# Two sums in two banks for the convolution's taps, in a decoder layer that runs at TensorE's pace

## The chip, the core and the metric

The kernel runs on one core of one Trainium2 chip. The metric is the device time of one execution in microseconds. In the profile PE is TensorE's matmuls and PEld its weight loads, DVE is VectorE, ACT ScalarE, POOL GpSimd, SP SyncE.

## What is computed

One decoder layer on a sequence of 512 positions with 1024 features: a half-step feed-forward layer, a token mixer, a second half-step feed-forward layer and a gated embedding. The mixer joins a sliding-window attention with a convolution branch. The change lies in the branch's depthwise convolution, 31 taps back in time, each channel by itself:

```python
ca, cb = jnp.split(zc, 2, axis=-1)
u = ca * jax.nn.sigmoid(cb)
u = causal_depthwise_conv(u, dw_w[i], dw_b[i])
c = jax.nn.silu(layernorm(u, conv_ln_g[i], conv_ln_b[i])) @ conv_proj[i]
...
merged = jax.nn.sigmoid(ga) * a + jax.nn.sigmoid(gb) * c
x = x + merged @ w_out[i]
```

For a feature f the convolution is y[f, s] = b[f] + sum over d from 0 to 30 of w[30 - d, f] * u[f, s - d], with zeros ahead of the sequence.

## The kernel before

Activations lie feature by position: eight tiles of 128 features (partitions) by 512 positions, called channels 0 to 7 below. A weight matrix comes in pieces of 128x1024, each split into a high and a low part by ScalarE and VectorE (`whi_`, `wlo_`), and each product takes three matmuls (high times high, low times high, high times low). A projection of one output tile is thus 24 matmuls of 512 columns into one PSUM bank.

The kernel is first recorded and then planned. `record()` writes the program down as operations on named tiles without places. `simulate()` then plays the operations through with a cost for each (`costs`) and gives every tile a place and every operation a start; `plan()` does this several times with different due times and keeps the shortest. Each engine then gets its instructions in the order of those starts (`hybrid_layer`, where line 1778 issues all of them, so that every row of the profile bears that line). A change to some operations thus makes a new order for all engines, and the order is fixed once the kernel is built. The written list `ORDER` gives the sequence in which the mixer's steps are recorded: `a` and `b` are the two projections of a convolution channel (tiles `ca`, `cb`), `K` and `Q` keys, values and queries, `A`, `E`, `V` scores, softmax and values of a query block, `g` and `h` the two gates (`ga`, `gb`), `p` the attention's output projection (`ap`), `L` the normalization behind the convolution. The projection `cp` reads what `L` leaves. The queries of the first eight heads come from `query_unit` with the seven-product form of `unit` and turned operands (tiles `wq_a`, `wq_b`), the other eight from a plain projection (`q1b`).

PSUM has eight banks, each 128 x 512 float32, class `ps` in the planner. A projection holds one while it sums, a group of scores takes four at once (`sc`), each transpose (`qTp`, `pT`) one, the plain query projection four.

The convolution of a channel starts when its gate is through (`conv_gate`, which makes `u`). Channels 0, 2 and 4 (`POOLCH`) are summed by GpSimd in SBUF, with ScalarE scaling each tap (tiles `ct`). Channels 1, 3, 5, 6 and 7 are summed by VectorE in a PSUM bank (`cz`): tap 0 with the bias by a `tensor_scalar`, taps 2 to 30 each by a `scalar_tensor_tensor` that reads the bank and writes it back, a copy of column 0, and at last tap 1, whose result goes to the SBUF tile `ys`. The class of `cz` tiles has a limit of two banks in use (`CAPS`). A tile can have a `mate`; the planner then opens both together:

```python
need.setdefault(vt.cls, {})[vt] = True
if vt.mate:
    need[vt.cls][vt.mate] = True
...
if len(free[c]) < len(vts) + spare:
    return False
if any(vt.kind and inuse[vt.kind] + (vt.mate is not None) >= CAPS[vt.kind] for vt in vts):
    return False
```

`conv_norm` (step `L`) adds the eight `ys` tiles (`ln_acc`), splits the sum (`ln_s`), takes the mean over features with a matmul (`ln_mb`), then the variance (`ln_v`), and splits the normalized tiles for `cp` (`cv_h`, `cv_l`).

Of the kernel before, what the change touches and what calls it, by code (L numbers as in the profile page):

```python
# [9 lines left out]
F32 = mybir.dt.float32  # L10
F32R = mybir.dt.float32r
I32 = mybir.dt.int32
AF = mybir.ActivationFunctionType
ALU = mybir.AluOpType
AX = mybir.AxisListType

P = 128
S = 512
# [10 lines left out]
TAPS = 31  # L29
PAD = TAPS - 1  # L30
# [14 lines left out]
POOLCH = (0, 2, 4)  # L45
# [643 lines left out]
def record():  # L689
    nc = Program()  # L690
# [4 lines left out]
    def ftile(name):  # L695
        return nc.tile(name, [P, S], F32, "a")
# [205 lines left out]
    g_ffn1, g_mix, g_ffn2, g_gate, g_ple, dwb, lng, lnb = (g_all[:, i] for i in range(8))  # L902
# [32 lines left out]
    dww = nc.tile("dww", [P, KD, TAPS], F32, "c")  # L935
# [301 lines left out]
    def halves(tag, key, i, h, cuts):  # L1237

        w = piece(key, i)
        out = []  # L1240
        for c in range(cuts):
            v = slice(c * S // cuts, (c + 1) * S // cuts)
            out.append(ps_tile(f"{tag}_{c}"))
            with nc.group(f"{tag}_{c}"):
                for k in range(KD):
                    mm3(out[c][:, v], part(w, slice(k * P, (k + 1) * P)), part(h[k], v), k == 0, k == KD - 1)
        return out
# [14 lines left out]
    us, ys, pas = [None] * KD, [None] * KD, [None] * KD  # L1262
# [4 lines left out]
    def conv_gate(c):  # L1267
        pb = proj(f"cb{c}", "wzc", 2 * c + 1, h2)
        sg = ftile(f"sg{c}")
        nc.vector.tensor_tensor(sg, pb, rb2, op=ALU.mult)  # L1270
        nc.scalar.activation(sg, sg, AF.Sigmoid)
        nc.gpsimd.tensor_tensor(sg, sg, rb2, op=ALU.mult)
        us[c] = ftile(f"u{c}")
        nc.vector.tensor_tensor(us[c], pas[c], sg, op=ALU.mult)
        conv(c)
# [3 lines left out]
    def conv(c):  # L1279
        u = us[c]  # L1280
        ys[c] = ftile(f"y{c}")
        ext = c not in POOLCH
        y = nc.tile(f"cz{c}", [P, S], F32, "ps") if ext else ys[c]
        nc.vector.tensor_scalar(
            y, u, dww[:, c, PAD:TAPS], dwb[:, c : c + 1], op0=ALU.mult, op1=ALU.add
        )
        for d in [*range(2, TAPS), 1] if ext else range(1, TAPS):
            wk = dww[:, c, PAD - d : TAPS - d]
            yd, ud = y[:, d:S], u[:, 0 : S - d]
            if not ext:  # L1290
                t = ftile(f"ct{c}_{d}")[:, 0 : S - d]
                nc.scalar.activation(t, ud, AF.Copy, scale=wk)
                nc.gpsimd.tensor_tensor(yd, yd, t, op=ALU.add)
            elif d == 1:
                nc.vector.tensor_copy(ys[c][:, 0:1], y[:, 0:1])
                nc.vector.scalar_tensor_tensor(ys[c][:, d:S], ud, wk, yd, op0=ALU.mult, op1=ALU.add)
            else:
                nc.vector.scalar_tensor_tensor(yd, ud, wk, yd, op0=ALU.mult, op1=ALU.add)


    def heads_rsqrt(tag, zs, n, scale, psum):
# [392 lines left out]
    for oo in range(1):  # L1694
# [6 lines left out]
        for f, m, b1, b2 in steps:  # L1701
            o = 2 * oo + m
            if f == 1:
                t, u = gt[m] = ftile(f"gt{o}"), ftile(f"gt{o + 4}")
# [4 lines left out]
            elif f == 6:  # L1709
                t, u = gt[m]  # L1710
                nc.scalar.copy(t[:, hi_], b2)
                nc.scalar.copy(u[:, hi_], b1)
            elif f == 7:
                t, u = gt[m]
# [6 lines left out]
            else:  # L1721
                t, u = gt[m]
                nc.vector.scalar_tensor_tensor(u[:, lo_], b2, -1.0, rb4[:, lo_], op0=ALU.mult, op1=ALU.mult)
                gate(o + 4, u, lo_)
    for i, o in enumerate((2, 3, 6, 7)):
        ps = halves(f"pg{o}", "wgate", 4 + i, h4, 2 if o == KD - 1 else 1)
# [169 lines left out]
```

## Time and profile before

| what | value |
|---|---|
| median of 3 runs | 1145.6 us (1145.52 to 1145.76) |
| profiled execution | 1145.5 us, span 1143.8 us |
| busy PE / PEld | 1135.7 / 1054.2 us |
| busy DVE / ACT / POOL | 1000.4 / 743.0 / 457.8 us |
| mean granted TensorE clock | 0.999 |
| the taps on VectorE | from 389.8 to 618.8 us of the span |

Busy time of an engine is the time in which it has at least one instruction in execution. Matmul records overlap, so the pitch from one matmul's start to the next says more than PE's busy share. Times in the lists below are microseconds from the span's start; a row of the timeline gives the start, the duration (of a run of like instructions where it ends in xN), the engine and the operation, and in brackets how long the engine sat idle before it and what ended that.

### The profile page before, as it was taken

The numbers are of one execution on the slowest core, as the hardware profiler recorded it, in microseconds if no ns is written. First come the engines' busy times: TensorE is split into PE (matmuls) and PEld (weight loads), VectorE is DVE, ScalarE is ACT, GpSimd is POOL, SyncE is SP. The second block draws the span as 40 slices with busy tenths as digits, with TensorE's granted clock in tenths as the row PEclk, the third lists the DMA queues.
The fourth block names the chain that finished last, engine by engine and source line by source line (L and its number), as shares of the span: only waits on it lengthen the run. The fifth ranks groups of instructions, "written<-read, shape, count | busy, mean of one in ns | idle before, by whom it ended". The sixth has DMA issues, their size and how long they took to land.

```text
span 1143.8 us, 20799 instructions
## 1 busy us (share of the span) xinstructions
PE 1135.7 (99%) x7804; PEld 1054.2 (92%) x7804; DVE 1000.4 (87%) x1701; ACT 743.0 (65%) x1332; POOL 457.8 (40%) x531
## 2 busy tenths in 40 slices
PE   9999999999999999999999999999999999999998
PEld 8899999999999988888888888988999999999997
DVE  7799978889887799997997779989998788899897
ACT  7656456665557889999975654655663566565682
POOL 1632113322112896976688124035231132131156
PEclk9999999999999999999999999999999999999999
DMA  7456666665658481664644554436666666656643
GB/s 242 126 162 148 165 160 163 151 144 151 157 132 208 119 206 38 173 158 97 162 129 131 146 148 108 114 108 169 145 164 151 150 167 148 168 119 178 152 117 99
DMA packets 54821, 167.92 MB, mean 147 GB/s; under 512 B 6592, under 2 KB 14400, under 8 KB 54720
## 3 DMA queue, kind: packets, MB, share of 16 engines
q1 hardware_dynamic: 39888, 114.12, 30.2%
q0 software_dynamic: 14688, 52.44, 26.6%
q8 instruction: 61, 1.00, 0.4%
q14 instruction: 40, 0.33, 0.1%
q10 hardware_dynamic: 144, 0.03, 0.0%
HBM read 145.59 MB, written 2.10 MB: 129 GB/s over the span
## 4 chain that ended last, share of the span: by engine, by line
PE 97%; DVE 3%; issue 0%; ACT 0%; ACTq 0%
PE wgu_b L1778 17%; PE wgu_a L1778 13%; PE wd_b L1778 10%; PE wd_a L1778 8%; PE f_g L1778 5%; PE f_u L1778 5%; PE gb L1778 4%; PE ga L1778 4%; PE ap L1778 4%; PE cp L1778 4%; PE ca L1778 3%; PE cb L1778 3%; PE wout_b L1778 2%; PE pg L1778 2%; PE q1b L1778 2%; PE wout_a L1778 2%
## 5 line engine op out<-in xcount | busy, mean ns | idle before, releaser
L1778 DVE TENSOR_TENSOR wlo_wgu<-raw_wgu,whi_wgu 128x1024 fp32r<-128x1024 f32 (+1 forms) x141 | 140.4, 1010 | 27.1 <-ACT whi_wgu L1778 26.8
L1778 ACT ACTIVATE whi_wgu<-raw_wgu 128x1024 fp32r<-128x1024 f32 (+1 forms) x141 | 115.4, 838 | 69.8 <-PE wgu_b L1778 34.7
L1778 POOL TENSOR_TENSOR y<-y,ct 128x511 f32<-128x511 f32 (+26 forms) x90 | 112.0, 1319 | 14.1 <-ACT ct L1778 5.3
L1778 PE MATMUL wgu_b<-f_t_h,wlo_wgu 128*128 128x256 f32 x408 | 115.5, 283 | 0.0
L1778 PE MATMUL wgu_b<-f_t_h,whi_wgu 128*128 128x256 f32 x408 | 115.5, 283 | 0.0
L1778 PE MATMUL wgu_b<-f_t_l,whi_wgu 128*128 128x256 f32 x408 | 115.5, 283 | 0.0
L1778 ACT ACTIVATE whi_wd<-raw_wd 128x896 fp32r<-128x896 f32 (+1 forms) x60 | 59.3, 989 | 73.3 <-PE wd_b L1778 41.5
L1778 DVE SCALAR_TENSOR_TENSOR cz<-u,dww,cz 128x504 f32<-128x504 f32 (+28 forms) x145 | 104.7, 733 | 2.0
L1778 POOL DMA_DIRECT2D raw_wgu<-in_wgu x34 | 29.7, 878 | 153.3 <-DMA raw_wgu<-in_wgu 78.6
L1778 PEld LDWEIGHTS wgu_b<-f_t_h,wlo_wgu 128*128 128x128 f32 x408 | 78.3, 192 | 0.0
L1778 PEld LDWEIGHTS wgu_b<-f_t_h,whi_wgu 128*128 128x128 f32 x408 | 78.3, 192 | 0.0
L1778 PEld LDWEIGHTS wgu_b<-f_t_l,whi_wgu 128*128 128x128 f32 x408 | 78.3, 192 | 0.0
L1778 DVE TENSOR_TENSOR wlo_wd<-raw_wd,whi_wd 128x896 fp32r<-128x896 f32 (+1 forms) x60 | 70.8, 1180 | 7.2 <-ACT whi_wd L1778 6.8
L1778 PE MATMUL wgu_a<-f_nh,wlo_wgu 128*128 128x256 f32 x272 | 77.0, 283 | 0.0
L1778 PE MATMUL wgu_a<-f_nh,whi_wgu 128*128 128x256 f32 x272 | 77.0, 283 | 0.0
L1778 PE MATMUL wgu_a<-f_nl,whi_wgu 128*128 128x256 f32 x272 | 77.0, 283 | 0.0
L1778 PE MATMUL wd_b<-f_f_h,wlo_wd 128*128 128x256 f32 x264 | 75.1, 285 | 1.2 <-DVE x L1778 1.2
L1778 PE MATMUL wd_a<-f_f_h,wlo_wd 128*128 128x256 f32 x264 | 74.7, 283 | 0.0
L1778 PE MATMUL wd_a<-f_f_h,whi_wd 128*128 128x256 f32 x264 | 74.7, 283 | 0.0
L1778 PE MATMUL wd_b<-f_f_l,whi_wd 128*128 128x256 f32 x264 | 74.7, 283 | 0.0
L1778 PE MATMUL wd_b<-f_f_h,whi_wd 128*128 128x256 f32 x264 | 74.7, 283 | 0.0
L1778 PE MATMUL wd_a<-f_f_l,whi_wd 128*128 128x256 f32 x264 | 74.7, 283 | 0.0
(625 smaller groups left out, 4278.6 us busy)
## 6 DMA issues: line engine op xcount, KB each, us to landing
raw_wgu<-in_wgu SPq DMA_DIRECT2D x76, 512.0 KB, 4.5
raw_wgu<-in_wgu POOLq DMA_DIRECT2D x34, 512.0 KB, 5.5
raw_wd<-in_wd SPq DMA_DIRECT2D x32, 448.0 KB, 4.0
raw_wd<-in_wd SPq DMA_DIRECT2D x16, 512.0 KB, 4.4
raw_wzc<-in_wzc SPq DMA_DIRECT2D x16, 512.0 KB, 3.9
wlo_wzc<-raw_wzc POOLq DMA_DIRECT2D x16, 512.0 KB, 4.9
raw_wzg<-in_wzg SPq DMA_DIRECT2D x16, 512.0 KB, 3.5
wlo_wzg<-raw_wzg POOLq DMA_DIRECT2D x16, 512.0 KB, 4.5
```

What stands on the lines that cost most here:

```text
L1778: made[op] = getattr(engines[op.eng], op.what)(*a, **k)
```

## The change

The five VectorE channels get two PSUM tiles each, `ya` and `yb`, mates of each other. Even taps go to `ya` (tap 0 opens it with the bias), odd taps to `yb` (tap 1 opens it by a `tensor_scalar` with 0 added), in the order 0, 1, 2, 4, 5, ... 30, 3. Tap 3, the last, writes its result to `ys` instead of the bank. Then two small copies bring columns 1 and 2 of `yb` and column 0 of `ya` into `ys`, and a `tensor_tensor` adds `ya` to `ys`. A channel has 34 instructions in place of 32. The branch for channels 0, 2 and 4 is written out apart, with the same operations as before. With a limit of two `cz` banks, mates can only be opened when no other channel holds one.

```diff
     def conv(c):
         u = us[c]
         ys[c] = ftile(f"y{c}")
-        ext = c not in POOLCH
-        y = nc.tile(f"cz{c}", [P, S], F32, "ps") if ext else ys[c]
-        nc.vector.tensor_scalar(
-            y, u, dww[:, c, PAD:TAPS], dwb[:, c : c + 1], op0=ALU.mult, op1=ALU.add
-        )
-        for d in [*range(2, TAPS), 1] if ext else range(1, TAPS):
+        if c in POOLCH:
+            y = ys[c]
+            nc.vector.tensor_scalar(y, u, dww[:, c, PAD:TAPS], dwb[:, c : c + 1], op0=ALU.mult, op1=ALU.add)
+            for d in range(1, TAPS):
+                t = ftile(f"ct{c}_{d}")[:, 0 : S - d]
+                nc.scalar.activation(t, u[:, 0 : S - d], AF.Copy, scale=dww[:, c, PAD - d : TAPS - d])
+                nc.gpsimd.tensor_tensor(y[:, d:S], y[:, d:S], t, op=ALU.add)
+            return
+        ya, yb = (nc.tile(f"cz{c}{n}", [P, S], F32, "ps") for n in "ab")
+        ya.vt.mate, yb.vt.mate = yb.vt, ya.vt
+        for d in [*range(3), *range(4, TAPS), 3]:
+            y = (ya, yb)[d % 2]
             wk = dww[:, c, PAD - d : TAPS - d]
             yd, ud = y[:, d:S], u[:, 0 : S - d]
-            if not ext:
-                t = ftile(f"ct{c}_{d}")[:, 0 : S - d]
-                nc.scalar.activation(t, ud, AF.Copy, scale=wk)
-                nc.gpsimd.tensor_tensor(yd, yd, t, op=ALU.add)
+            if d == 0:
+                nc.vector.tensor_scalar(yd, ud, wk, dwb[:, c : c + 1], op0=ALU.mult, op1=ALU.add)
             elif d == 1:
-                nc.vector.tensor_copy(ys[c][:, 0:1], y[:, 0:1])
-                nc.vector.scalar_tensor_tensor(ys[c][:, d:S], ud, wk, yd, op0=ALU.mult, op1=ALU.add)
+                nc.vector.tensor_scalar(yd, ud, wk, 0.0, op0=ALU.mult, op1=ALU.add)
             else:
-                nc.vector.scalar_tensor_tensor(yd, ud, wk, yd, op0=ALU.mult, op1=ALU.add)
+                to = ys[c][:, d:S] if d == 3 else yd
+                nc.vector.scalar_tensor_tensor(to, ud, wk, yd, op0=ALU.mult, op1=ALU.add)
+        nc.vector.tensor_copy(ys[c][:, 1:3], yb[:, 1:3])
+        nc.vector.tensor_copy(ys[c][:, 0:1], ya[:, 0:1])
+        nc.vector.tensor_tensor(ys[c][:, 1:S], ya[:, 1:S], ys[c][:, 1:S], op=ALU.add)
```

## The prediction

> **What bounds the kernel now.** I read the page's first part and its chain first, then the windows of the stage in which the convolution runs, then what the weight loads of TensorE waited for.
>
> ```profile
> span 1143.8 us, 20799 instructions
> PE 1135.7 (99%) x7804; PEld 1054.2 (92%) x7804; DVE 1000.4 (87%) x1701; ACT 743.0 (65%) x1332; POOL 457.8 (40%) x531
> PE 97%; DVE 3%; issue 0%; ACT 0%; ACTq 0%
> ...
> L1778 DVE TENSOR_SCALAR cz<-u,dww,g_all x5: 799/803/806, 389.8 to 584.9; 128x512 f32<-128x512 f32 x5
> L1778 DVE COPY y<-cz x5: 157/157/159, 393.2 to 593.3; 128x1 f32<-128x1 f32 x5
> L1778 DVE SCALAR_TENSOR_TENSOR y<-u,dww,cz x5: 729/742/747, 436.0 to 618.1; 128x511 f32<-128x511 f32 x5
> ...
> 389.70:618.80 229.10, 227.96 (x1227) 190.41 (x1226) 214.20 (x386) 206.37 (x431) 184.07 (x239) 1.00 0.56 139
> 389.70:618.80 229.10, 112.52 (x160) 1.00 0.56 139
> ```
>
> The tile view of `cz` dates the stage: the first tap starts at 389.8, the last ends just before 618.8. In the windows over it (columns: PE, PEld, DVE, ACT, POOL, clock, DMA share, GB/s) PE is busy 227.96 of 229.10 us and VectorE 214.20, of which the second row, the same window for `cz` alone, gives the taps 112.52. So VectorE is the second busiest engine here, but the chain is 97% TensorE. Busy matmul records overlap, so I look at the pitch in the chain instead.
>
> ```profile
> 460.67 21.79 PE q1b L1778 x96
> 576.70 5.44 PE ga L1778 x24
> 661.10 43.52 PE cp L1778 x192
> ```
>
> 43.52/192 is 0.227 us for a matmul 512 wide; in the stage 5.44/24 and 21.79/96 are the same 0.227. TensorE runs at its own pace beside the taps, and what it loses stands in its waits:
>
> ```profile
> PEld wd_b L1778 <- DVE x L1778: 2.1, 4, 0.7
> PEld sc L1778 <- issue: 1.4, 4, 0.4
> PEld ca L1778 <- DVE s L1778: 1.1, 1, 1.1
> PEld sc L1778 <- DVE cz L1778: 0.4, 1, 0.4
> PEld pT L1778 <- POOL s L1778: 0.3, 1, 0.3
> PEld cb L1778 <- DVE s L1778: 0.3, 1, 0.3
> ```
>
> Three waits in the stage can go: `ca` 1.1, `cb` 0.3, `pT` 0.3, together 1.7 us. The `sc` waits, 0.4 us each whoever is named (the `cz` row is one of them), come before score groups and follow no particular engine; I leave them. `wd_b` lies outside the stage. **So a faster convolution has 1.7 us to win in its own stage, 0.15% of the run.** A difference of 0.2% (2.3 us) is about what a measurement of this kernel tells from no change.
>
> **The change part by part.** Before, five channels (1, 3, 5, 6, 7) each sum 31 taps in one bank; a tap reads what the tap before it wrote. What that costs is seen by comparing two runs of taps. Channel 3 opens only at 417.37, so the run at 401.50 is one channel in one bank; at 475.95 channels 3 and 5 take turns in two.
>
> ```profile
> 401.50 5.40 DVE L1778 SCALAR_TENSOR_TENSOR cz<-u,dww,cz 128x502 f32<-128x502 f32 x7
> 417.37 0.80 DVE L1778 TENSOR_SCALAR cz<-u,dww,g_all 128x512 f32<-128x512 f32 x1
> 473.57 0.80 DVE L1778 TENSOR_SCALAR cz<-u,dww,g_all 128x512 f32<-128x512 f32 x1
> 475.95 6.46 DVE L1778 SCALAR_TENSOR_TENSOR cz<-u,dww,cz 128x486 f32<-128x486 f32 x10
> ```
>
> With 0.74 us for the last record of each, same bank: (5.40 - 0.74)/6 = 0.777 us from start to start; by turns: (6.46 - 0.74)/9 = 0.636. The dependence costs 0.14 us a tap. It costs that only where a tap directly follows a tap of its own bank; behind any other instruction the wait is already covered. I count 60 such followers in the stage, the first and the last of them in these rows:
>
> ```profile
> 390.60 0.76 DVE L1778 SCALAR_TENSOR_TENSOR cz<-u,dww,cz 128x510 f32<-128x510 f32 x1
> 618.05 0.75 DVE L1778 SCALAR_TENSOR_TENSOR y<-u,dww,cz 128x511 f32<-128x511 f32 x1
> ```
>
> Removed: with turns, one same-bank follower is left in each channel (tap 4 behind tap 2), so 55 x 0.14 = 7.7 us of VectorE time go.
>
> Added to each channel: a second TENSOR_SCALAR in place of a tap, one more small COPY, and the closing addition of the two sums. The addition reads one bank and one SBUF tile and writes SBUF, like `u<-ca,sg`:
>
> ```profile
> 393.24 0.16 DVE L1778 COPY y<-cz 128x1 f32<-128x1 f32 x1
> 393.43 0.75 DVE L1778 SCALAR_TENSOR_TENSOR cz<-u,dww,cz 128x508 f32<-128x508 f32 x1
> 415.94 0.68 DVE L1778 TENSOR_TENSOR u<-ca,sg 128x512 f32<-128x512 f32 x1
> 416.54 0.18 DVE L1778 SCALAR_TENSOR_TENSOR q_y<-q_rs,q_y 128x32 f32<-128x32 f32 x1
> 584.92 0.80 DVE L1778 TENSOR_SCALAR cz<-u,dww,g_all 128x512 f32<-128x512 f32 x1
> 585.64 2.65 DVE L1778 SCALAR_TENSOR_TENSOR cz<-u,dww,cz 128x483 f32<-128x483 f32 x4
> ```
>
> From start to start: addition 416.54 - 415.94 = 0.60, TENSOR_SCALAR 585.64 - 584.92 = 0.72 less the tap it replaces 0.64, copy 393.43 - 393.24 = 0.19. That is 0.60 + 0.08 + 0.19 = 0.87 a channel; the addition may also wait 0.14 for the copy before it. Five channels: 4.4 us, at most 5.1. Tap 3 writing to `ys` instead of the bank is the old last tap's form (742 ns in the tile view), no change.
>
> Net on VectorE: 4.4 - 7.7 = **-3.3 us** in 229 (-2.6 with the extra waits, +4.4 if turns gained nothing). On the path: nothing directly, since TensorE's 228 us cover it. If that cover were gone the gain would be at most the 1.7 us of waits. POOL and ScalarE do the three other channels as before; no DMA and no matmul is added or removed.
>
> The Trainium skill, Advanced Engine Details and Errata, The Read-Write Bubble, says that memory latency shows as a bubble between instructions, and makes no difference between banks. By that rule alone the turns would save nothing and VectorE's sum would be +4.4 instead of -3.3; the trace here, 0.777 against 0.636, speaks for a part that depends on the bank.
>
> What the change takes is room. A channel now opens two of the eight banks together, and the code lets it open only when no other channel holds one. Before, one bank was held from 389.8 to 618.8, and two only while neighbours overlapped:
>
> ```profile
> 435.99 0.75 DVE L1778 SCALAR_TENSOR_TENSOR y<-u,dww,cz 128x511 f32<-128x511 f32 x1
> 482.32 0.74 DVE L1778 SCALAR_TENSOR_TENSOR y<-u,dww,cz 128x511 f32<-128x511 f32 x1
> 589.45 0.73 DVE L1778 SCALAR_TENSOR_TENSOR y<-u,dww,cz 128x511 f32<-128x511 f32 x1
> ```
>
> That is 417.37 to 436.7, 473.57 to 483.1, 584.92 to 590.2: 34 us. After, two are held nearly all the time. A group of scores takes four banks at once, and PE's order is fixed, so a missing bank stops everything behind the group. No row shows such a wait as it will be. Below it may be a gain: the three waits go, -1.7. Above, each of the eight score groups waits once as `ca` does at 428.83, for the copies out of score banks:
>
> ```profile
> 428.34 0.77 DVE L1778 COPY_PREDICATED s<-masks,sc 128x256 f32<-128x256 int32 x2
> 428.83 0.19 PEld L1778 LDWEIGHTS ca<-mix_h_h,wlo_wzc 128*128 128x128 f32 x1 [1.12 <-DVE s L1778]
> ```
>
> 8 x 1.1 = +8.8. The copies that free a score bank are short, and six banks hold four scores, a transpose and a projection; so I take the low side, one wait like that of `cb`, +0.3.
>
> **The sum.** The profiled execution took 1145.5 us (span 1143.8 and 1.7 around it), the three runs have a median of 1145.6. 1145.6 + 0 (taps, covered) + 0.3 = 1145.9 us.
>
> **The rivals.**
> *Slower: score groups wait for banks.* For it: the order of the whole kernel is worked out anew at build from a model of costs, with one bank fewer for TensorE in this stage, and the order before leaves TensorE so little idle time that any new order is more likely to add than to take. Against it: with two channels open, 417 to 437, TensorE still kept its pace outside the one wait. It decides from the third wait of 1.1 us on (2.3 us in all); four of them give 1150.0, eight 1154.4. The Trainium skill, Perfetto Trace Analysis, Matmul Optimizations, wants all eight banks in use for parallel work of TensorE, which speaks for this rival.
>
> *Slower: the channels end late.* A channel waits until two banks are free together and the channel before has ended, so the last sum may come late for the normalization:
>
> ```profile
> 618.83 0.69 DVE L1778 TENSOR_TENSOR ln_acc<-ln_acc,y 128x512 f32<-128x512 f32 x1
> 625.00 0.69 DVE L1778 TENSOR_TENSOR ln_s_l<-ln_acc,ln_s_h 128x512 fp32r<-128x512 f32 x1 [3.74 <-ACT ln_s_h L1778]
> 630.94 0.39 PE L1778 MATMUL ln_mb<-ln_s_h,mean_r 128*128 128x512 f32 x1
> 662.67 1.30 DVE L1778 TENSOR_TENSOR cv_l<-y,cv_h 128x512 fp32r<-128x512 f32 x2 [0.24 <-ACT cv_h L1778]
> ```
>
> The sum's split is ready at 625.7 and its matmul comes at 630.9: 5.2 us of slack. Behind it there is little, the last `cv_l` ends at 664.0 when `cp` has run since 661.1. Each us beyond 5.2 is idle TensorE time; a last sum 10 us late gives 4.8, so 1150.4, and from 7.5 us late it decides. Against it: channels 6 and 7 hold many of the 60 followers and become shorter.
>
> *Faster.* VectorE's shorter queue removes all three waits: 1145.6 - 1.7 = 1143.9, still within 0.2%. More needs also the `wd_b` waits outside the stage (2.1): 1141.8. Nothing in the change reaches them but the new order.
>
> *The change doesn't do what it says.* If turns within one channel keep the pitch of 0.777, VectorE has 4.4 us more in a stage where it idles 229.1 - 214.2 = 14.9: again 1145.9, with a wait or two.
>
> **How the numbers follow.** Same, with or without the tap gain: 0.56 (0.46 and 0.10). Banks: 0.26. Late end: 0.12. Faster by over 0.2%: 0.06. So faster 0.06, same 0.56, slower 0.38, and the time is that of the same case, 1145.9, whose own range is 1143.9 to 1147.9. The range reaches down to 1143.9 (three waits gone), leaving 0.07 below, and up to 1151.5, five waits of 1.1 and a little more, leaving 0.12 above.
>
> **What would show it.** Taps at a pitch near 0.64 us with no run at 0.78; 170 records in the five channels against 160 (34 each: 2 TENSOR_SCALAR, 29 taps, 2 copies, 1 addition); VectorE in the stage some 3 us less busy; TensorE's 0.227 unchanged. The banks' rival would show as waits of `sc` or the projections above 0.4 us on VectorE's or ScalarE's reads of scores; the late end as idle TensorE before `ln_mb` or `cp`. I am wrong if the stage's waits of PEld for other engines come to 4 us or more, or if TensorE loses time in a stage that has no taps because the new order is worse there.

## The result, and the profile after

The changed kernel takes 1152.79 us (median of four runs, 1152.54 to 1153.1), the kernel before beside it 1145.67 (1145.52 to 1145.76). The ratio is 1.0062 with a 95% interval of 1.0045 to 1.008: slower by 7.1 us. The forecast was 1145.9 with a range up to 1151.5, and no difference as the likeliest case; the time lies 1.3 us above that range.

First the lines of the page that answer to those of before (span; busy time of the engines; chain of work that ended last):

```profile
span 1150.8 us, 20811 instructions
PE 1138.3 (99%) x7804; PEld 1054.0 (92%) x7804; DVE 1003.0 (87%) x1711; ACT 748.3 (65%) x1336; POOL 456.6 (40%) x531
PE 86%; DVE 6%; ACT 6%; issue 0%; DMA 0%; ACTq 0%; DVEq 0%
```

TensorE has the same 7804 matmuls and is 99% busy by its records as before, but its share of the chain fell from 97% to 86%, and 6% each went to VectorE and ScalarE: the chain now passes through them. These shares are not TensorE's waits, which come to a few us and are read below. The place is found by the start of `cp` in the chain of the changed kernel:

```profile
668.18 43.52 PE cp L1785 x192
```

Before it was 661.10, with the same 43.52 us. So the whole loss (7.0 us of span, 7.08 by this row) lies ahead of `cp`, and what follows is unchanged. The windows (columns PE, PEld, VectorE, ScalarE, GpSimd, clock, DMA share, GB/s) narrow it down; before:

```profile
0.00:389.80 389.80, 388.05 (x2865) 371.80 (x2866) 331.64 (x588) 235.39 (x423) 111.90 (x145) 1.00 0.62 159
389.80:450.00 60.20, 59.06 (x367) 50.38 (x366) 59.39 (x118) 54.88 (x121) 48.98 (x68) 1.00 0.59 142
450.00:500.00 50.00, 50.00 (x267) 41.51 (x266) 46.67 (x85) 49.65 (x99) 45.73 (x65) 1.00 0.57 141
500.00:570.00 70.00, 70.00 (x384) 57.99 (x381) 61.46 (x125) 69.32 (x167) 45.37 (x71) 1.00 0.58 141
```

and after:

```profile
0.00:389.80 389.80, 387.96 (x2864) 371.63 (x2865) 331.81 (x587) 235.10 (x423) 111.91 (x145) 1.00 0.62 159
389.80:450.00 60.20, 59.38 (x369) 50.56 (x368) 59.81 (x119) 53.84 (x109) 51.49 (x68) 1.00 0.58 143
450.00:500.00 50.00, 46.67 (x230) 37.32 (x230) 49.44 (x86) 49.64 (x106) 45.48 (x66) 1.00 0.52 125
500.00:570.00 70.00, 68.63 (x385) 56.21 (x384) 59.37 (x119) 68.70 (x164) 47.68 (x73) 1.00 0.57 138
```

Up to the first tap nothing differs. From 450 to 500 TensorE lacks 3.3 us and from 500 to 570 1.4 us, where before it lacked none. Idle records are not the whole loss: a matmul can start late while the record before it still runs, since the records overlap. For every matmul I took the time to the next one's start, less the usual pitch of its shape (0.227 us for 512 columns, 0.120 for 256, 0.109 for a transpose). From 400 to 600 us the sum of this excess is 7.0 us larger after than before; 4.9 of it stands behind transposes (`pT`, `qTp`), 1.9 behind matmuls 512 wide.

The waits of TensorE in the stage (what waited, for whom, us, times, longest) were one row before:

```profile
PE ca L1778 <- DVE s L1778: 0.9, 1, 0.9
```

After there are nine, 5.4 us together, all of which follow:

```profile
PE pT L1785 <- ACT zq L1785: 1.0, 1, 1.0
PE o L1785 <- DVE sgb L1785: 0.9, 1, 0.9
PE qTp L1785 <- DVE of L1785: 0.8, 1, 0.8
PE qTp L1785 <- DVE q_rs L1785: 0.6, 1, 0.6
PE pT L1785 <- DVE s L1785: 0.6, 2, 0.3
PE cb L1785 <- DVE of L1785: 0.5, 1, 0.5
PE q1b L1785 <- DVE s L1785: 0.4, 1, 0.4
PE ca L1785 <- DVE s L1785: 0.4, 1, 0.4
PE o L1785 <- DVE p_l L1785: 0.2, 1, 0.2
```

Read each row by whether the named result is an operand. `pT` transposes `s`, not `zq`; `qTp` and `cb` don't read `of`; `q1b` and `ca` don't read `s`; `o` does not read `sgb`. What these have in common is that the named instruction reads a PSUM bank (`zq` reads `q1b`, `sgb` reads `gb`, `of` reads `o`, `s` reads `sc`), and the matmul that waits is the next to write in a bank. Six rows, 4.0 us, are thus what a wait for a bank looks like. The plan of the changed kernel says which bank each tile has (`vt.slot`), and it confirms them: in each of the six rows the tile that waits opens the bank that the named instruction is the last to read. By the same numbers the row `pT` <- `s` belongs to them, although `pT` does read `s`: both times the transposes open a bank of scores from another query block. That makes 4.6 us. The other two rows (`q_rs`, `p_l`), 0.8 us, fit operands of the queries and of the softmax that come late. One of the first kind in the timeline:

```profile
484.07 1.82 ACT L1785 ACTIVATE zq<-q1b,mix_n_r 128x512 f32<-128x512 f32 x3
484.88 1.20 PE L1785 MATMUL pT<-ident,s 128*128 128x128 f32 x8 [0.99 <-ACT zq L1785]
```

ScalarE empties the query projection's banks, and the transposes begin when one of them is read.

### The profile page after: what moved, and what is told of

Read it like the earlier page. It is cut to its first block, busy times and chain, and to the rows that moved or that the text cites. A ratio compares the mean times of both kernels' runs of the same rounds, so it can differ in the third digit from the quotient of the medians.

```text
span 1150.8 us, 20811 instructions
## 1 busy us (share of the span) xinstructions
PE 1138.3 (99%) x7804; PEld 1054.0 (92%) x7804; DVE 1003.0 (87%) x1711; ACT 748.3 (65%) x1336; POOL 456.6 (40%) x531
## 4 chain that ended last, share of the span: by engine, by line
PE 86%; DVE 6%; ACT 6%; issue 0%; DMA 0%; ACTq 0%; DVEq 0%
PE wgu_b L1785 17%; PE wgu_a L1785 13%; PE wd_b L1785 10%; PE wd_a L1785 8%; PE f_g L1785 5%; PE f_u L1785 5%; PE ap L1785 4%; PE cp L1785 4%; PE gb L1785 3%; PE ga L1785 2%; ACT s L1785 2%; PE wout_b L1785 2%; PE ca L1785 2%; PE pg L1785 2%; PE cb L1785 2%; PE wout_a L1785 2%
## 5 line engine op out<-in xcount | busy, mean ns | idle before, releaser
L1785 POOL TENSOR_TENSOR y<-y,ct 128x505 f32<-128x505 f32 (+27 forms) x90 | 111.0, 1270 | 14.6 <-ACT ct L1785 7.6
L1785 POOL TENSOR_TENSOR f_f_ta<-f_us 128x256 f32<-128x256 f32 x22 | 25.5, 1161 | 96.9 <-DVE f_us L1785 79.9
```

What stands on the lines that cost most here:

```text
L1785: made[op] = getattr(engines[op.eng], op.what)(*a, **k)
```

## The experiments

Four theories stood against each other. *Bank*: a second bank held by the convolution takes places from TensorE. *Order*: any edit here makes a new order for all engines, and a new order is worse whatever the edit. *Taps*: the tap instructions by turns disturb VectorE's queue. *Late end*: with two banks a channel, one channel at a time, the sums come late. All times are medians, with the kernel before run on the same chip beside them.

**The old taps, with an idle second bank.** One sum a channel as before, but a second `cz` tile is opened with it and written once at the end.

```diff
+        if ext:
+            idle = nc.tile(f"cz{c}i", [P, S], F32, "ps")
+            y.vt.mate, idle.vt.mate = idle.vt, y.vt
...
+                nc.vector.tensor_copy(idle[:, 0:1], ys[c][:, 1:2])
```

> The kernel before, one sum in one bank, with a second bank opened and held beside it as a mate and touched only by one extra copy of one column behind the last tap; so two banks a channel, one channel at a time, the old taps. If the missing bank is what costs (theory bank): most of the 7.1 us come back, 1150 to 1154, with waits of PEld on VectorE's reads of other groups' banks. If the new taps and the closing addition cost (theory taps): 1145.6 within 1 us. If the new order alone is unlucky (theory order): no lean, anywhere from 1144 to 1152.

1154.76 against 1145.64, ratio 1.008 (1.0065 to 1.0095). Holding the bank, with the new order that this makes, costs 9.1 us, more than the whole change and just above what the theory of the bank had named. The loss does not need the new taps, so the theory of the taps falls as its cause. Two of the waits of its weight loads:

```profile
PEld pT L1782 <- POOL s L1782: 5.0, 9, 2.5
PEld o L1782 <- DVE p_l L1782: 1.5, 2, 0.8
```

They stand again at the attention's transposes and values, not at the scores, and the longest is for GpSimd's scaling of the softmax, not for a reader of a bank.

**One channel at a time.** The kernel before with a limit of one `cz` bank.

```diff
-CAPS = {"cz": 2, "ct": 4, "zs": 2, "zt": 2}
+CAPS = {"cz": 1, "ct": 4, "zs": 2, "zt": 2}
```

> The kernel before with the limit of convolution banks set from two to one: one bank, one channel at a time. If the cost of the change is that channels no longer overlap (a rival, late end): slower than before by 3 us or more, 1148.5 and up. If it is the number of banks held: no slower than before, 1143.5 to 1146.5, since TensorE gets a bank more while channels overlapped.

1145.60 against 1145.64, ratio 1.0 (0.9991 to 1.001). Channels one after the other cost nothing, though this too made a new order. So a new order need not cost.

**The sequence of TensorE exchanged.** Each kernel was built with TensorE's groups in a given sequence and with due times from that plan; the other engines are planned as ever. In `before_oa` one sum follows the sequence of the changed kernel, in `after_ob` two sums follow the sequence of before.

```diff
-WINDOW = 10
+WINDOW = 1
...
+    prog.groups = [made[i] for i in GROUPS]
+    when = {}
+    for g, t in zip(prog.groups, STARTS):
```

> The kernel before, one sum in one bank, but TensorE's groups in the sequence that the changed kernel has; the other engines are planned to it. Theory bank: waits for banks shrink, at least 3 of the 7.1 us are gone, 1146 to 1149.5. Theory order: the sequence is what costs, 1151.5 to 1154.

> The changed kernel, two sums in two banks, but TensorE's groups in the sequence of the kernel before. Theory order: the cost goes with the sequence, 1145 to 1148. Theory bank: groups that stood where seven banks were free now wait, 1151 or more.

One sum in the changed kernel's sequence: 1150.26, ratio 1.004 (1.0025 to 1.0055). Two sums in the sequence of before: 1153.35, ratio 1.0063 (1.0047 to 1.008). Neither sequence saves the two sums, and the new one, with the planning that goes with it, costs the old convolution 4.6 us. `before_oa` fell between the two theories and decides nothing, and `after_ob` lies where the theory of the bank put it. But these builds lack their own controls, so these came later: each kernel with its own sequence given.

> A control for the two runs with a given sequence: the kernel before with its own sequence of TensorE's groups given in the same way, the other engines planned to it anew. If giving the sequence costs nothing: 1145 to 1147. If it costs by itself: 1148 or more, and the two runs say less.

> The changed kernel with its own sequence of TensorE's groups given, the other engines planned anew; the fourth corner beside one sum with either sequence (1150.5 and 1150.3) and two sums with the sequence of before (1153.4). Theory bank: 2 us or more above 1150.3. Theory order: 1149 to 1151.

`before_ob` (one sum, the sequence of before, written down) takes 1150.51 against 1145.75, ratio 1.0042 (1.0027 to 1.0057): with nothing changed in the convolution or in TensorE's sequence, planning the other engines anew under these due times costs 4.8 us. So the two runs above say less when they are held against the kernel before, and have to be read against this control. `after_oa` takes 1152.57 against 1145.66, ratio 1.006 (1.0043 to 1.0076), the changed kernel's own time: there the same planning anew costs nothing. So the 4.8 us are no fee for planning again; the order of before is a good one that the new planning does not find. There are now two pairs with the same sequence of TensorE, due times and method, one sum against two: +2.8 us in the sequence of before (1153.35 - 1150.51), +2.3 in that of the changed kernel (1152.57 - 1150.26). The waits of TensorE in the second pair show it; one sum:

```profile
PE q1b L1852 <- DVE s L1852: 1.4, 1, 1.4
PE qTp L1852 <- DVE of L1852: 0.5, 1, 0.5
PE o L1852 <- DVE p_l L1852: 0.2, 1, 0.2
```

and two sums, the three longest of eight rows:

```profile
PE pT L1859 <- ACT zq L1859: 1.0, 1, 1.0
PE qTp L1859 <- POOL zq L1859: 0.9, 1, 0.9
PE o L1859 <- DVE p_l L1859: 0.7, 1, 0.7
```

2.1 us of waits become 4.9 over all rows, +2.8 for +2.3 of time. Matmuls wait for `zq` with two sums only, though a weight load waits for it with one sum as well (0.7 us, against 1.1 with two).

**Two sums in some channels.** `two167` leaves channels 3 and 5, whose taps lie beside the attention, with one sum; `two3` gives two sums to channel 3 alone.

```diff
+TWO = (1, 6, 7)
...
+        if c not in TWO:
+            y = nc.tile(f"cz{c}", [P, S], F32, "ps")
```

> Two sums in two banks for channels 1, 6 and 7 alone; channels 3 and 5, which run beside the attention's scores, keep one sum in one bank. Theory bank: the room is there where these three run, so 1145 to 1147. Theory taps (new instructions cost wherever they stand): three fifths of the 7.1 us stay, about 1149.9.

> Two sums in two banks for channel 3 alone, the other four as before. Theory bank: one channel beside the scores is enough for half of the 7.1 us or more, 1149 to 1153. Theory taps: one fifth, about 1147.0.

1151.78, ratio 1.005 (1.0035 to 1.0065), and 1152.10, ratio 1.0057 (1.0041 to 1.0074). The first was a miss for both theories: the bank wanted it near the kernel before, the taps at 1149.9. Most of its loss comes from one wait in another place, outside the attention:

```profile
PE ap L1798 <- DVE wlo_wap L1798: 2.0, 1, 2.0
...
627.80:631.00 3.20, 1.17 (x6) 0.67 (x5) 2.93 (x2) 1.06 (x1) 2.78 (x4) 1.00 0.88 164
631.00:633.00 2.00, 2.00 (x8) 1.53 (x7) 0.64 (x1) 0.63 (x1) 0.67 (x1) 0.62 1.04 195
633.00:635.00 2.00, 2.00 (x7) 1.56 (x6) 0.06 (x1) 0.00 (x0) 0.00 (x0) 0.53 1.03 223
```

TensorE idles 2.0 us for a split of weights that VectorE made late, and then its clock is granted at 0.62 and 0.53 in the next two windows of 2 us. About 4 of its 6 us are this one accident of the order (the one of its four runs with a mean clock of 1.0 took 1150.21 us). `two3`, where a single channel costs nearly as much as five, lies where the theory of the bank put it, but has a 3.1 us wait of its own:

```profile
429.61 0.74 DVE L1798 SCALAR_TENSOR_TENSOR cz3a<-u,dww,cz3a 128x506 f32<-128x506 f32 x1
430.26 1.10 DVE L1798 COPY_PREDICATED s<-masks,sc 128x256 f32<-128x256 int32 x3
430.75 0.50 PE L1798 MATMUL ca<-mix_h_h,wlo_wzc 128*128 128x512 f32 x1 [3.12 <-DVE s L1798]
```

The copy that frees a score bank was ordered behind a run of channel 3's taps on VectorE, and `ca` waited for the bank. That is the wait of 1.1 us that the prediction quoted, three times as long. The cost does not grow with the number of channels, as a price of the bank alone would; each build also has the accidents of its own order.

**The order without the bank.** `hold2_free` is planned as `hold2`; then the copies into the idle banks are dropped, and the eight banks are given out again, the longest free first, with every engine's order kept.

```diff
+    prog.ops = [o for o in prog.ops if not (o.writes and o.writes[0].vt.name.startswith("cz") and o.writes[0].vt.name.endswith("i"))]
...
+        vt.slot = until.index(min(until))
```

> The order of all engines as in the run that held an idle second bank (1154.8), but the idle bank is not held and its five copies are left out: the other tiles are spread over all eight banks, the longest free first. If the cost is matmuls that wait at run time for a bank: most of the 9.1 us go, 1146 to 1149. If the cost is in the order that was made under the shortage (scores later, so softmax and transposes later): 1152 to 1155.

1155.08 against 1145.75, ratio 1.0081 (1.0066 to 1.0096): the bank is back, the time is not. So in this build the price lies in the order that was planned without the bank, not in a wait for the bank on the chip. In the profiled run its longest wait, 2.97 us of transposes for GpSimd's scaling of the softmax, took the clock along:

```profile
463.03 2.43 PE L1799 MATMUL pT<-ident,s 128*128 128x128 f32 x8 [2.97 <-POOL s L1799]
...
460.00:470.00 10.00, 7.03 (x23) 5.24 (x23) 9.87 (x18) 9.92 (x21) 8.63 (x12) 0.66 0.35 113
```

That does not change the reading: the two runs with a mean clock of 0.999 took 1154.51 and 1154.76 us, as long as `hold2`.

**Other written orders.** Two lists drawn at random (a few steps of `ORDER` moved by some places), each with one sum and with two:

```diff
 list1
-K0 a0 b0 a1 b1 Q0 A0 a3 a2 A1 b2 E0 E1 b3 A2 E2 a4 V0 A3 a5 E3 V1 b4 Q1 V2 b5
-V3 A5 a7 A6 g5 h7 A4 E5 A7 E6 E4 V6 g3 a6 E7 g0 V5 b6 V4 g4 g6 V7 h1 g2 h4 b7
+K0 a0 b0 a1 b1 Q0 A0 a3 a2 A1 b2 E0 E1 b3 V0 A2 E2 a4 A3 a5 E3 V1 b4 Q1 V2 b5
+V3 A5 a7 A4 A6 g5 h7 E5 A7 E6 E4 V6 g3 a6 E7 g0 V5 b6 V4 g4 g6 V7 h1 g2 h4 b7
...
 list2
+K0 a0 b0 a1 b1 Q0 A0 a3 a2 A1 b2 E0 E1 b3 A2 E2 a4 V0 A3 a5 E3 V1 b4 V3 Q1 V2
```

> The kernel before with three steps of its written list moved by a few places, drawn at random (V0 and A4 earlier, p1 later); one sum in one bank. It is the partner of the next run. Theory order: a moved list alone costs some us, 1147 to 1153. Theory bank: near the old time, 1145 to 1148.

> The changed kernel with the same moved list. Theory bank: slower than its partner by 2 us or more. Theory order: the difference to the partner is of either sign, within 4 us.

> A second drawn list (V3 and p1 earlier, p7 later), one sum in one bank. Theory order: 1147 to 1155. Theory bank: 1145 to 1148.

> The changed kernel with the second list. Theory bank: slower than its partner by 2 us or more. Theory order: either sign, within 4 us.

| list | one sum | two sums | difference |
|---|---|---|---|
| list1 | 1150.36, 1.0039 (1.0024 to 1.0055) | 1156.47, 1.0092 (1.0062 to 1.0121) | +6.1 |
| list2 | 1158.54, 1.011 (1.008 to 1.0139) | 1160.05, 1.0123 (1.0094 to 1.0152) | +1.5 |

The ratios are against the kernel before. In list1 the difference is what the theory of the bank asked for (2 us or more); in list2 it is not. The differences also hold some clock, since three of the four builds ran at 0.997 or less on the mean and list1 with one sum at 0.998 or more. A random list costs the kernel before 4.3 and 12.5 us; the second is above the range of either theory. In list2 with one sum a single wait carries half of it:

```profile
PE pT L1778 <- POOL s L1778: 6.6, 2, 6.4
...
465.00:475.00 10.00, 3.36 (x10) 1.94 (x9) 6.13 (x13) 9.90 (x31) 7.32 (x12) 0.50 0.46 105
```

**Lists searched for each.** For one sum, two sums and one sum with a limit of one bank, a list was searched by the planner's own forecast of the span. For two sums it reads:

```diff
-K0 a0 b0 a1 b1 Q0 A0 a3 a2 A1 b2 E0 E1 b3 A2 E2 a4 V0 A3 a5 E3 V1 b4 Q1 V2 b5
...
+K0 a0 b0 a1 Q0 A0 b1 a3 A1 a2 E0 E1 b2 b3 A2 a4 E2 V0 b4 A3 V1 E3 a5 Q1 V2 b5
+V3 a7 A6 g5 h7 A5 E6 A4 A7 E5 E4 a6 E7 g0 V4 V6 b6 V5 h4 g4 g3 g6 V7 g2 h1 b7
+p0 g1 p2 g7 p3 L0 p4 h5 p6 p1 h3 p7 h0 h6 h2 p5
```

> The changed kernel, with a written list of steps that was searched for it (the planner's own forecast of the whole, over some 450 lists). If two banks cost in themselves, whatever the order: 1149 or more. If a good order can hide them: 1145 to 1148.

> The kernel before with a list searched in the same way and for as long. If the list of before was already about the best: 1145 to 1147. If the search finds something: 1143.5 to 1145. The difference to the run above is what two banks cost with an order made for each.

> One bank and one channel at a time, with a list searched for it in the same way. A candidate to beat both kernels: 1143 to 1145.5; if the planner's forecast misses what a new order costs on the chip: 1146 to 1150.

Against 1145.66: two sums 1148.74, ratio 1.0026 (1.0016 to 1.0036); one sum 1147.02, ratio 1.001 (1.0001 to 1.002); limit of one 1145.19, ratio 0.9996 (0.9987 to 1.0006). A searched list gives back 4.0 of the 7.1 us, which lies between the two answers that were put down ahead. It does not reach one sum under the same search (+1.7), nor the kernel before (+3.1). For one sum the search made the kernel slower than its old list did, by 1.4 us, so the planner's forecast does not pick the best list. The longest waits left with two sums:

```profile
PE ap L1785 <- ACT oT10h L1785: 1.2, 1, 1.2
PE qTp L1785 <- DVE of L1785: 0.8, 1, 0.8
PE o L1785 <- DVE s L1785: 0.8, 1, 0.8
```

No version beats the kernel before by more than a measurement can tell; 1145.19 lies within it.

## Why the prediction was wrong, step by step

**The ledger of VectorE held.** The pitch of taps by turns was put at 0.64 us:

```profile
403.11 0.73 DVE L1785 SCALAR_TENSOR_TENSOR cz1a<-u,dww,cz1a 128x500 f32<-128x500 f32 x1
403.75 0.73 DVE L1785 SCALAR_TENSOR_TENSOR cz1b<-u,dww,cz1b 128x497 f32<-128x497 f32 x1
404.39 0.73 DVE L1785 SCALAR_TENSOR_TENSOR cz1a<-u,dww,cz1a 128x498 f32<-128x498 f32 x1
...
616.71 0.14 DVE L1785 COPY y<-cz7b 128x2 f32<-128x2 f32 x1
616.83 0.16 DVE L1785 COPY y<-cz7a 128x1 f32<-128x1 f32 x1
616.90 0.68 DVE L1785 TENSOR_TENSOR y<-cz7a,y 128x511 f32<-128x511 f32 x1
617.50 1.21 DVE L1785 TENSOR_TENSOR wlo_wap<-raw_wap,whi_wap 128x1024 fp32r<-128x1024 f32 x1
```

404.39 - 403.11 over two taps is 0.64, and no two `scalar_tensor_tensor` taps in a row start more than 0.66 us apart. The closing addition takes 0.60 as put; the two copies take 0.12 and 0.07, together what one copy was given. Over the 170 instructions of the five channels, the times to the next start on VectorE (no longer than the record) sum to 105.1 us, against 107.2 for the 160 before: -2.1. With pauses of up to 0.1 us behind a record counted in, as in the predicted pitch of 0.777, it is 106.1 against 110.4: -4.2. The predicted -3.3 lies between. The expected fall of VectorE's busy time by 3 us was not to be seen, though: it is 1003.0 against 1000.4, because the same 1541 other instructions fill 4.7 us more in the new order. A saving in one group is read from that group, not from the engine's sum. One reading of the prediction goes too far: that the cost of the old taps depends on the bank. They also read what the tap just before wrote, and that is enough, as the last section shows.

**The pace of TensorE held.** `cp` still has 43.52/192 = 0.227 us. The taps never were on the path, and the old taps with the bank held were slower still (1154.76).

**The three waits did not go.** Of the 1.7 us that a faster convolution had to win, `ca`, `cb` and `pT` wait again for `s` and `of`, and further waits came beside them.

**The step that failed: "one wait like that of `cb`, +0.3".** Two things were wrong in it. It priced the missing bank as a wait of a fixed sequence, with room for "four scores, a transpose and a projection" in six banks. The five pairs (+2.8 and +2.3 with the same sequence of TensorE, +6.1 and +1.5 with the same list, +1.7 with a list searched for each) put the two sums at 2.9 us on the mean, all on one side, though the intervals of single pairs mostly overlap. That this is the bank and not the taps is inferred: the old taps with a bank held are no faster (`hold2`), and the waits stand where banks come free. And it left the new order out of the sum, which it had named itself under a rival: the order of before leaves TensorE 0.9 us of waits in the stage, and planning it again with nothing changed costs 4.8 us (`before_ob`). 2.9 for the bank leaves about 4 of the 7.1 for the order; this is a remainder, not a measurement, and it is near those 4.8. The planner itself could have been asked. The span that `simulate()` forecasts is 1144.2 us for the kernel before and 1148.3 for the changed one, so +4.1 stood in the two sources ahead of any run. The bounds of -1.7 and +8.8 did hold the truth; the value between them was taken at the wrong end, and the stated range ended at 1151.5.

**The rival "score groups wait for banks" had the right size and the wrong place.** It gave 1150.0 to 1154.4, and the measured time lies in it by luck. For the waits of `sc` stayed at 0.4 us each, eight of them, as before: the planner doesn't open a group of scores before its banks are free, it puts other work ahead of it. The late work is what comes behind: transposes, values, queries. The Trainium skill, Perfetto Trace Analysis, Matmul Optimizations, wants all eight PSUM banks in use, for the most parallel work. The five pairs agree: with one bank fewer for TensorE each is slower, by 1.5 to 6.1 us.

**"The channels end late" is false.** The last sum ends at 617.6 us, before at 618.8, and the kernel with one channel at a time is not slower. **The sign that I had named for being wrong was there:** the weight loads' waits for other engines in the stage, those of `sc` left out, sum to 6.0 us, where 4 was the mark. The longest:

```profile
PEld o L1785 <- ACT p_h L1785: 1.1, 1, 1.1
PEld qTp L1785 <- POOL q_w L1785: 1.0, 1, 1.0
PEld q1b L1785 <- DVE s L1785: 0.9, 1, 0.9
```

What stays open: how the 2.9 us divide into waits on the chip (4.6 of the 5.4 us of waits are for banks) and a worse plan (the build with the bank given back is no faster). The planner, which knows the banks but not the chip's own delays, forecasts +4.8, +1.2, +5.8, +2.8 and +0.9 us for the five pairs in the order above. So a worse plan alone has the size and the side of the measured differences, while the single values miss by up to 2 us. The exchange of sequences and the lists sample a handful of orders; the spread of the pairs, 1.5 to 6.1, says how little one of them alone would have shown.

## What to carry to other kernels

Where one engine runs at its own pace through a stage and a planner fits the rest around it, price an edit by what it takes from that engine (banks, places), and give a term of its own to the order being made anew: plan the unchanged kernel again and see what that costs. Ask the planner for its forecast of both versions first; here it said +4.1 of the 7.1 us. Compare such edits only in pairs with the same order, and in more than one order. A saving on an engine that is covered was worth nothing here, and the PSUM bank that was paid for it made a loss.

## What the runs showed of the hardware

A tap on VectorE that reads what the instruction just before it wrote started after the end of that record, a tap by turns before the end: taps of one sum in a row were 0.777 us apart with records of 0.74 us, taps by turns 0.64 with records of 0.73 (some 500 columns). No shared bank is needed for this: `ln_acc` reads the last `y` from SBUF and starts at 618.83, 0.03 us behind the end of the tap that wrote it (618.05 + 0.75, both rows stand in the prediction).

The clock of TensorE does not follow the length of one idle gap. In `two167` a gap of 2.03 us, in a stretch of 3.2 us with 1.17 us busy, was followed by a clock of 0.62 and 0.53, and the matmuls of `ap` went from 0.227 to 0.43 us apart:

```profile
632.02 0.63 PE L1798 MATMUL ap<-oT02h,wlo_wap 128*128 128x512 f32 x1
632.45 0.63 PE L1798 MATMUL ap<-oT02h,whi_wap 128*128 128x512 f32 x1
```

In `two3` a gap of 3.12 us, in a stretch of 4 us with 0.88 us busy, left it at 1.00:

```profile
427.00:431.00 4.00, 0.88 (x7) 0.64 (x6) 4.00 (x9) 3.96 (x10) 3.78 (x5) 1.00 1.01 240
431.00:435.00 4.00, 4.00 (x18) 3.24 (x18) 4.00 (x10) 3.97 (x12) 0.28 (x1) 1.00 0.12 23
```

The clock records of the traces tell more. The stretches at half clock last 3.41 us (`two167`, from 631.47), 6.83 (`hold2_free`), 10.24 (`list2_two`) and 13.65 us (`list2_one`), whole multiples of 3.41. Counted in steps of 3.41 us from the first rise to full clock, the gap of `two167` lies whole in the step ahead of the fall (628.06 to 631.47), while that of `two3` is cut at 428.96 into 1.33 and 1.79 us. That the idle time within one step decides fits both cases; no run was made to test it.

The Trainium skill, TensorE: Matmul & The Clock Gate, Part 1, lets the clock fall to half after an idle window of about 3.4 us, and the window runs freely. The steps in the traces agree with the window. That 2.03 us idle within one step were enough is less than the page asks for there, and the measurement decides.
